# High and low parts of a stationary operand side by side, element by element, in the two gate-and-up stages of a decoder layer on one Trainium2 core

## The chip, the cores and the metric

The kernel runs on one core of one Trainium2 chip, in one launch. The metric is the device time of one execution in microseconds. Two runs of the kernel before took 2149.1 and 2149.21 us, with a median of 2149.15 us.

## The reference

One decoder layer on 256 tokens of width 2048, with 16 learned tokens put in front (272 positions). It has two SwiGLU feed-forward blocks around a mixer of attention and short convolution. Cut to what matters here:

```python
D_MODEL, SEQ, N_META, D_FF = 2048, 256, 16, 5632

def swiglu_ffn(h, w_gu, w_down):
    gate, up = jnp.split(h @ w_gu, 2, axis=-1)
    return (jax.nn.silu(gate) * up) @ w_down

    h = rms_norm(s, norm_ffn1)
    s = s + 0.5 * swiglu_ffn(h, ffn1_w_gu, ffn1_w_down)       # 272 positions
    ...                                                       # mixer, merged with w_gate, w_branch, w_out
    h = rms_norm(s, norm_ffn2)
    s = s + 0.5 * swiglu_ffn(h, ffn2_w_gu, ffn2_w_down)       # 256 positions are kept
    s = rms_norm(s, norm_final)
```

All inputs are float32, and the matrices `w_gu` are 2048 x 11264 in each feed-forward block.

## The kernel before, in words

**Products in two parts.** Every operand X of a large product is held as a high part (X rounded to the format float32r) and a low part (X less the high part, in the same format). A product A·B is three matmuls into one accumulator: high·high, low·high, high·low. ACT writes the high part of a weight tile (a copy that rounds), DVE subtracts it from the tile for the low part.

A matmul has a stationary operand of 128 x 128, loaded into the array before it, and a moving operand of 128 rows and up to 512 columns, streamed past it. In the trace each matmul is a pair: a weight load (PEld) and the matmul (PE). The load of the next matmul starts with the matmul that runs.

**First feed-forward block** (`gate_up`, L482, over `linear`, L305). The activations h1 move (272 columns, transposed: features on partitions), the weights are stationary. h1 is an `Act` (L174): eight tiles with two 128-row chunks each, in a tile the order is chunk, high or low, column. Each piece has room for 320 columns (`PIECE`), and the 272 sit at its end, so they start at column 48. The groups of 512 gate columns ("pg") and 512 up columns ("pu") alternate, 11 times each. One `linear` has 16 chunks; for each of them four blocks of 128 weight columns, and for each block three matmuls: L367 (high weights, high h1), L368 (high weights, low h1), L369 (low weights, high h1). Weights come 1 MB (four chunks) at a time by a DMA of SP's queue (L337), and are split two chunks at a time, one ACT copy of 128 x 1024 (L351) and one DVE subtraction (L356), into the tiles `wh` and `wl`. There are three buffers of each. So ACT waits until TensorE is done with the oldest one; nothing else sets the order there. The evictions of one linear run inside the next one (`flush` after its second chunk).

The down projection ("pd") is a `linear` too. Its activations are an `Apart` (L194): high and low parts in separate tiles of four chunks, 272 columns each, and its weight tiles start 16 or 48 columns into their buffers, with a chunk every 528 columns (`weights`, L209), so that weights and activations step in the same way.

**Second feed-forward block** (`gate_up_mix`, L686, over `linear_mix`, L549). Here the weights move (512 columns) and the activations h3 are stationary. h3 (L1100) is an `Act` as well, eight tiles for the eight pairs of chunks, 256 columns, without a lead: tiles 0 to 3 in buffers of 1088 columns (tag "act"), 4 to 7 in buffers of 1280 columns (tag "big"). A plan says for each pair of chunks which of two ways it goes: "D", eight products of a block of h3 with a weight tile, or "S", seven products as in Strassen's scheme, three of which take a block of h3 and four a sum of blocks (`sum_of_parts`, L523, and `combine`, L530, make these sums from the two parts). The plans are

```python
FFN2_FIRST = ("DDDDSSDS", (1,), {(3, 0): 4, (3, 1): 5, (6, 0): 7}, (4, 5))
FFN2 = ("DDSDSSDS", (1,), {(1, 1): 2, (3, 0): 4, (3, 1): 5, (6, 0): 7}, (2, 4, 5))
```

the first for the first of eleven groups, the second for the ten others. Each product is again three matmuls, L569 (high h3), L570 (low h3), L571 (high h3 with the low weights). The accumulators are "pg1" to "pg7" and "pgx", under the names pg and pgx in the trace.

h3 is made during the output projection ("pd" again in the names, 1356 to 1444 us): `turned` (L1117) transposes two chunks into PSUM, ACT multiplies by the gain into the high part (L1127), DVE makes the low part (L1128).

**The order of the work.** It is written out by hand in lists: `side` and `later` are taken at fixed chunks, `ahead` keeps the weight splits of `linear_tok` and `linear_mix` two tiles ahead of their products. None of it has costs or due times, and the change touches none of it.

Of the kernel before, what the change touches and what calls it, by code (L numbers as in the profile page):

```python
# [9 lines left out]
F32 = mybir.dt.float32  # L10
F32R = mybir.dt.float32r
# [4 lines left out]
P = 128  # L16
D = 2048
SEQ = 256
NMETA = 16
T = SEQ + NMETA  # L20
F = 5632
DC = D // P
GC = 4
GW = GC * P
W2 = D // 2
NH = 8
# [9 lines left out]
N_BIG = 8  # L36
PIECE = 320
# [17 lines left out]
DOWN = ("DDSDSDSD", (), {(1, 1): 2, (3, 1): 4, (5, 1): 6}, ())  # L55
DOWN_LAST = ("DDDSDS", (1,), {(2, 1): 3, (4, 1): 5}, ())
AHEAD = 2


@with_exitstack  # L60
def decoder_layer(ctx: ExitStack, tc: tile.TileContext, t, out):
    nc = tc.nc

    const = ctx.enter_context(tc.tile_pool(name="const", bufs=1))
    wpool = ctx.enter_context(tc.tile_pool(name="w", bufs=W_BUFS))
    apool = ctx.enter_context(tc.tile_pool(name="a", bufs=N_ACT))
# [4 lines left out]
    def bank(name):  # L71
        return psum.tile([P, 512], F32, tag="acc", name=name)
# [45 lines left out]
    def load_vectors():  # L118
# [12 lines left out]
        out=mask[:, T - P :],  # L131
        in_=mask[:, T - P :],
# [41 lines left out]
    class Act:  # L174


        def __init__(self, name, chunks, width, wide_slots=(), piece=None):
            self.width, self.lead = width, 0 if piece is None else piece - width
            self.tiles = []
            for g in range(chunks // 2):  # L180
                if g in wide_slots:
                    w = piece or width
                    raw = apool.tile([P, 4 * PIECE], F32R, tag="big", bufs=N_BIG, name=f"{name}{g}")
                    self.tiles.append(raw[:, : 4 * w].rearrange("p (c l w) -> p c l w", c=2, l=2))
                else:
                    self.tiles.append(apool.tile([P, 2, 2, width], F32R, tag="act", name=f"{name}{g}"))

        def both(self, c, t0, t1):
            return self.tiles[c // 2][:, c % 2, :, self.lead + t0 : self.lead + t1]

        def part(self, c, lo, t0, t1):
            return self.tiles[c // 2][:, c % 2, lo, self.lead + t0 : self.lead + t1]

    class Apart:  # L194

# [99 lines left out]
    def step(use, ring=True):  # L295

        ahead.append((use, ring))
        while sum(r for _, r in ahead) > AHEAD:
            ahead.pop(0)[0]()

    def drain():
        while ahead:
            ahead.pop(0)[0]()

    def linear(act, chunks, w, k0, c0, t0, t1, name, evict, before=None, side_at=(5, 9, 13), after=None, later_at=LATER_AT):  # L305

        n = t1 - t0
        kb = KB  # L310
        nl = LB * kb
        starts = list(range(0, len(chunks), kb))
        if before is not None:
            starts.insert(1, 1)
        acc = [bank(f"{name}_{j}") for j in range(GC)]
        ready = {}
        for b, b1 in zip(starts, starts[1:] + [len(chunks)]):
            blk = chunks[b:b1]
            r0 = (k0 + blk[0]) * P
            if isinstance(act, Apart):  # L320
                wh, wl = (
                    act.weights(wpool.tile([P, 2 * act.step + 2 * NMETA], F32R, tag=nm, name=nm), blk[0])
                    for nm in ("wh", "wl")
                )
            else:
                wh = wpool.tile([P, kb, GW], F32R, tag="wh", name="wh")
                wl = wpool.tile([P, kb, GW], F32R, tag="wl", name="wl")
            m = len(blk)
            if before is not None or b % nl == 0:
                st = wpool.tile([P, LB * kb, GW], F32, tag="st", bufs=ST_BUFS, name="st")  # L330
                ml = m if before is not None else min(nl, len(chunks) - b)
                with ExitStack() as order:
                    for ins in x_load:
                        order.enter_context(tc.issue_after(ins))
                    x_load.clear()
                    last_load[:] = [
                        nc.sync.dma_start(  # L337
                            out=st[:, :ml, :],
                            in_=w[r0 : r0 + ml * P, c0 : c0 + GW].rearrange("(c p) f -> p c f", p=P),
                        ).ins  # L340
                    ]
            sw = st[:, :m, :] if before is not None else st[:, b % nl : b % nl + m, :]
            with ExitStack() as order:
                if before is not None and b == 0:
                    with tc.issue_after(nc.scalar.copy(out=wh[:, :m, :], in_=sw).ins):
                        ready[0] = before(blk)
                if before is not None:
                    for ins in ready.pop(b):
                        order.enter_context(tc.issue_after(ins))
                if before is None or b:  # L350
                    nc.scalar.copy(out=wh[:, :m, :], in_=sw)  # L351
                if before is None and b:
                    for ins in ahead_of_split:
                        order.enter_context(tc.issue_after(ins))
                    ahead_of_split.clear()
                nc.vector.tensor_sub(wl[:, :m, :], sw, wh[:, :m, :].bitcast(F32))  # L356
            if before is not None and b1 < len(chunks):
                ready[b1] = before(chunks[b1 : starts[starts.index(b1) + 1] if b1 < starts[-1] else None])
            drain()
            for i, c in enumerate(blk):  # L360
                first, last = b + i == 0, b + i == len(chunks) - 1
                for j in range(GC):
                    a, f = acc[j][:, :n], slice(j * P, (j + 1) * P)
                    if 2 * n <= 512:
                        nc.tensor.matmul(acc[j][:, : 2 * n], wh[:, i, f], act.both(c, t0, t1), start=first, stop=False)
                    else:
                        nc.tensor.matmul(a, wh[:, i, f], act.part(c, 0, t0, t1), start=first, stop=False)  # L367
                        nc.tensor.matmul(a, wh[:, i, f], act.part(c, 1, t0, t1), start=False, stop=False)  # L368
                    nc.tensor.matmul(a, wl[:, i, f], act.part(c, 0, t0, t1), start=False, stop=last)  # L369
                if b + i == EVICT_AT:  # L370
                    flush()
                if b + i in later_at and later:
                    later.pop(0)()
                if b + i in side_at and side:
                    side.pop(0)()
                if after is not None:
                    after(b + i)
        flush()
        pending.append(lambda: evict(acc))

    def flush():
        while pending:
            pending.pop(0)()
# [123 lines left out]
    class Mixed:  # L507
# [7 lines left out]
        def sum(self, p, pool=None):  # L515

            f = tmp.tile([P, 2, SEQ], F32, tag="sc", name="sf")
            for k in range(2):
                c = 2 * p + k
                nc.vector.tensor_scalar_mul(f[:, k, :], s(c, NMETA), col(self.g0 + c))  # L520
            self.combine(p, f, pool)
# [189 lines left out]
        nc.vector.tensor_sub(tl[:, :, 1, :], f, tl[:, :, 0, :].bitcast(F32))  # L711


    h1 = Act("h1", DC, T, range(NH), PIECE)
    norm1 = Norm(0, "1")

    pm, split_of, turned = [], [], []
# [67 lines left out]
    for half in halves:  # L785
        m = gate_up(h1, half, t["ffn1_w_gu"][0], norm1, 0, before1 if half is halves[0] else None)
        if half is halves[0]:
            with tc.issue_after(last_load[0]):
                load_vectors()
        else:  # L790
            side.extend((make_vec, make_lam))
        for c in range(0, DC, GC):

            def down(pd, c=c, final=half is halves[-1]):
                for j in range(GC):
                    nc.vector.scalar_tensor_tensor(
                        out=s(c + j, 0), in0=pd[j][:, :T], scalar=0.5, in1=s(c + j, 0), op0=ALU.mult, op1=ALU.add
                    )
                    if final:
                        after1(c + j)  # L800

            linear(m, list(range(len(half) * GC)), t["ffn1_w_down"][0], half[0] * GC, c * P, 0, T, "pd", down)
# [265 lines left out]
    for d in range(D // GW):  # L1068
# [19 lines left out]
        if d < 2:  # L1088
            n = 3 * d
# [7 lines left out]
            side_at=(2, 5) if d == GC - 1 else range(2, NH),  # L1097
        )

    h3 = Act("h3", DC, SEQ, range(4, NH))  # L1100
    hn = Mixed(h3, G_FFN2, False)
    rtok3 = const.tile([P, 2], F32, name="rtok3")
    nss = const.tile([P, 2, 4], F32, name="nss")
# [139 lines left out]
    for half in thirds:  # L1243
        m = Act("m", len(half) * GC, SEQ, range(4))
# [3 lines left out]
        if final:  # L1248
            for q in range(2):
                nc.gpsimd.dma_start(  # L1250
                    out=gfin[q],
                    in_=t["norm_final"][q * W2 : (q + 1) * W2].rearrange("(o d) -> o d", o=1).to_broadcast([P, W2]),
                )
        ma = Mixed(m, 0, True)
        for u in range(2):
# [31 lines left out]
            chunks = list(range(len(half) * GC))  # L1287
# [43 lines left out]
```

## Time and profile before

| | |
|---|---|
| median of the runs | 2149.15 us (2149.1 and 2149.21) |
| span of the profiled execution | 2147.3 us |
| granted TensorE clock, mean | 0.999 |
| first feed-forward block, gate and up | 6.5 to 296.9 us and 439.8 to 676.6 us |
| second feed-forward block, gate and up | 1443.8 to 1612.9, 1698.2 to 1864.3, 1949.7 to 2074.0 us |
| DMA | 439.70 MB, mean 205 GB/s |

The execution that was profiled has no time of its own beside its span. The span is counted from the first to the last instruction of the program, and the runs' times are device times around it.

How to read the views: a row of grouped instructions has the line of the kernel, the engine, the operation, the tiles it writes and reads, the shape and the count; then the busy time in us and the mean duration of one in ns; then the idle time of the engine before them and what ended it. Matmuls overlap, so the duration of one (start to modelled end) is longer than the distance from one start to the next; that distance comes from a stretch of time and the number of matmuls that start in it. The counts of a table of stretches include instructions that reach over its edges.

### The profile page before, as it was taken

To read this page: it belongs to the slowest core of one execution; us is meant where nothing else is said; L and a number is where in the kernel's file an instruction comes from. 1 tells how busy PE (TensorE), PEld (TensorE's weight loads), DVE (VectorE), ACT (ScalarE), POOL (GpSimd) and SP (SyncE) were. 2 spreads that over 40 slices of the span, in tenths; PEclk is the share of its full clock that TensorE was granted. 3 is DMA by queue.
4 is the path that set the end of the run, shared out by engine and by line. 5 is a ranking of instruction groups with operands and counts; after the bars stand their busy time and mean duration, and the time that the engine had idled before them with its cause. 6 is when DMAs were issued, how large, how long until landed. Compare 5 with 4: busy or idle time off the path is not lost.

```text
span 2147.3 us, 33079 instructions
## 1 busy us (share of the span) xinstructions
PE 2137.4 (100%) x13202; PEld 1929.1 (90%) x13202; DVE 1611.9 (75%) x2139; ACT 1105.5 (51%) x1391; POOL 79.4 (4%) x89
## 2 busy tenths in 40 slices
PE   9999999999999999999999999999999999999998
PEld 9999999999999998899988888888888888888887
DVE  8555554445555668867887889889999899988998
ACT  6344443344333455545545555557665566555665
POOL 0000000000000000000000000001100111012100
PEclk9999999999999999999999999999999999999999
DMA  7555555555555555544455555668886999779963
GB/s 258 177 177 178 177 181 177 178 180 179 180 180 176 178 178 187 190 157 142 154 189 186 198 201 187 216 206 256 267 259 198 286 285 277 234 219 311 287 207 138
DMA packets 200544, 439.70 MB, mean 205 GB/s; under 512 B 10493, under 2 KB 11206, under 8 KB 200390
## 3 DMA queue, kind: packets, MB, share of 16 engines
q1 hardware_dynamic: 184022, 398.13, 54.9%
q0 software_dynamic: 15904, 38.80, 8.2%
q8 instruction: 103, 1.69, 0.3%
q10 hardware_dynamic: 464, 0.66, 0.1%
q14 instruction: 51, 0.42, 0.1%
HBM read 431.26 MB, written 2.10 MB: 202 GB/s over the span
## 4 chain that ended last, share of the span: by engine, by line
PE 98%; DVE 1%; DMA 0%; ACT 0%; issue 0%; SPq 0%; ACTq 0%
PE pg L569 6%; PE pg L571 6%; PE pg L570 6%; PE pd L369 4%; PE pd L367 4%; PE pu L367 4%; PE pu L368 4%; PE pu L369 4%; PE pd L368 4%; PE pg L367 4%; PE pg L368 4%; PE pg L369 4%; PE pd L571 4%; PE pd L570 4%; PE pd L569 4%; PE g L571 2%
## 5 line engine op out<-in xcount | busy, mean ns | idle before, releaser
L356 DVE TENSOR_TENSOR wl<-st,wh 128x1024 fp32r<-128x1024 f32 (+1 forms) x329 | 401.1, 1221 | 378.4 <-ACT wh L351 378.3
L351 ACT CAST wh<-st 128x1024 fp32r<-128x1024 f32 (+1 forms) x328 | 343.0, 1047 | 487.4 <-PE pu L368 151.0
L476 DVE TENSOR_TENSOR wl<-st,wh 128x1024 fp32r<-128x1024 f32 (+1 forms) x424 | 470.9, 1118 | 55.4 <-ACT wh L475 52.3
L475 ACT CAST wh<-st 128x1024 fp32r<-128x1024 f32 (+1 forms) x424 | 400.3, 970 | 208.8 <-PE pdx L570 60.5
L475 ACT CAST wh<-t 128x1024 fp32r<-128x1024 f32 x160 | 166.6, 1052 | 242.5 <-DVE t L609 162.3
L476 DVE TENSOR_TENSOR wl<-t,wh 128x1024 fp32r<-128x1024 f32 x160 | 193.8, 1222 | 56.3 <-ACT wh L475 51.7
L369 PE MATMUL pd<-mh,wl 128*128 128x272 f32 x704 | 203.1, 288 | 0.0
L367 PE MATMUL pd<-mh,wh 128*128 128x272 f32 x704 | 202.3, 287 | 0.0
L367 PE MATMUL pu<-h,wh 128*128 128x272 f32 x704 | 201.9, 287 | 0.0
L367 PE MATMUL pg<-h,wh 128*128 128x272 f32 x704 | 201.6, 287 | 0.2 <-ACT h L231 0.2
L369 PE MATMUL pu<-h,wl 128*128 128x272 f32 x704 | 201.7, 287 | 0.0
L368 PE MATMUL pu<-h,wh 128*128 128x272 f32 x704 | 201.7, 286 | 0.0
L368 PE MATMUL pg<-h,wh 128*128 128x272 f32 x704 | 201.2, 287 | 0.1
L368 PE MATMUL pd<-ml,wh 128*128 128x272 f32 x704 | 200.7, 285 | 0.0
L369 PE MATMUL pg<-h,wl 128*128 128x272 f32 x704 | 199.6, 287 | 0.1
L570 PE MATMUL pg<-wh,h 128*128 128x512 f32 x399 | 156.0, 391 | 0.0
L569 PE MATMUL pg<-wh,h 128*128 128x512 f32 x399 | 155.8, 390 | 0.0
L571 PE MATMUL pg<-wl,h 128*128 128x512 f32 x399 | 155.7, 391 | 0.0
L368 PEld LDWEIGHTS pd<-ml,wh 128*128 128x128 f32 x704 | 133.5, 190 | 0.0
L367 PEld LDWEIGHTS pg<-h,wh 128*128 128x128 f32 x704 | 132.6, 188 | 0.7 <-ACT h L231 0.4
L368 PEld LDWEIGHTS pg<-h,wh 128*128 128x128 f32 x704 | 132.6, 188 | 0.3 <-DVE h L232 0.3
L368 PEld LDWEIGHTS pu<-h,wh 128*128 128x128 f32 x704 | 132.6, 188 | 0.0
(391 smaller groups left out, 4839.6 us busy)
## 6 DMA issues: line engine op xcount, KB each, us to landing
st<-in_ffn_w_gu_dram SPq DMA_DIRECT2D x183, 512.0 KB, 6.0
st<-in_ffn_w_down_dram SPq DMA_DIRECT2D x88, 1024.0 KB, 5.1
st<-in_ffn_w_gu_dram SPq DMA_DIRECT2D x84, 1024.0 KB, 4.9
st<-in_w_in_dram SPq DMA_DIRECT2D x48, 1024.0 KB, 5.1
st<-in_w_gate_dram SPq DMA_DIRECT2D x64, 512.0 KB, 4.1
t<-in_ffn_w_gu_dram POOLq DMA_DIRECT2D x64, 512.0 KB, 7.0
st<-in_w_branch_dram SPq DMA_DIRECT2D x32, 512.0 KB, 4.5
st<-in_w_out_dram SPq DMA_DIRECT2D x16, 1024.0 KB, 5.2
```

The source lines that it names most:

```text
L351: nc.scalar.copy(out=wh[:, :m, :], in_=sw)
L356: nc.vector.tensor_sub(wl[:, :m, :], sw, wh[:, :m, :].bitcast(F32))
L367: nc.tensor.matmul(a, wh[:, i, f], act.part(c, 0, t0, t1), start=first, stop=False)
L368: nc.tensor.matmul(a, wh[:, i, f], act.part(c, 1, t0, t1), start=False, stop=False)
L369: nc.tensor.matmul(a, wl[:, i, f], act.part(c, 0, t0, t1), start=False, stop=last)
L475: part_last[:] = [nc.scalar.copy(out=wh, in_=src).ins]
L476: part_last.append(nc.vector.tensor_sub(wl, src, wh.bitcast(F32)).ins)
L569: nc.tensor.matmul(ps[k], hi, wh, start=first, stop=False)
L570: nc.tensor.matmul(ps[k], lo, wh, start=False, stop=False)
L571: nc.tensor.matmul(ps[k], hi, wl, start=False, stop=left[k] == 0)
```

## The change

The diff does four things.

1. In the up linears of the first block ("pu"), the weight tiles `wh` and `wl` have another content: one tile for each of the two chunks, and in it the high and the low part of each column next to each other. A stationary operand is then every second element of its tile (a step of 8 bytes). ACT copies and DVE subtracts once per chunk, with every second element written.
2. The eight tiles of h1 get leads of their own, 48, 0, 16, 32, 40, 8, 24 and 44 columns, instead of 48 for all.
3. The tiles of h3 get places: tiles 0 to 3 hold high and low parts element by element and start 0, 16, 32 and 48 columns into their buffers; tiles 4 to 7 keep their order and start 16, 32, 48 and 8 columns in. A column is 4 bytes.
4. `linear` loses the branch that put both parts of a narrow activation into one matmul, and names the two weight operands of a block first.

```diff
+LEADS = [48, 0, 16, 32, 40, 8, 24, 44]
+PLACES = [(0, True), (16, True), (32, True), (48, True), (16, False), (32, False), (48, False), (8, False)]
...
-        def __init__(self, name, chunks, width, wide_slots=(), piece=None):
-            self.width, self.lead = width, 0 if piece is None else piece - width
+        def __init__(self, name, chunks, width, wide_slots=(), piece=None, leads=None, places=None):
+            self.width = width
+            self.leads = leads or [0 if piece is None else piece - width] * (chunks // 2)
             self.tiles = []
             for g in range(chunks // 2):
-                if g in wide_slots:
+                if places is not None:
+                    first, mixed_parts = places[g]
+                    if g in wide_slots:
+                        raw = apool.tile([P, 4 * PIECE], F32R, tag="big", bufs=N_BIG, name=f"{name}{g}")
+                    else:
+                        raw = apool.tile([P, GC * T], F32R, tag="act", name=f"{name}{g}")
+                    raw = raw[:, first : first + 4 * width]
+                    how = "p (c w l) -> p c l w" if mixed_parts else "p (c l w) -> p c l w"
+                    self.tiles.append(raw.rearrange(how, c=2, l=2))
+                elif g in wide_slots:
...
         def part(self, c, lo, t0, t1):
-            return self.tiles[c // 2][:, c % 2, lo, self.lead + t0 : self.lead + t1]
+            lead = self.leads[c // 2]
+            return self.tiles[c // 2][:, c % 2, lo, lead + t0 : lead + t1]
...
+            elif name == "pu":
+                mixed_w = [wpool.tile([P, GW, 2], F32R, tag=nm, name=nm) for nm in ("wh", "wl")]
...
-                if before is None or b:
+                if name == "pu":
+                    for i in range(m):
+                        nc.scalar.copy(out=mixed_w[i][:, :, 0], in_=sw[:, i, :])
+                elif before is None or b:
                     nc.scalar.copy(out=wh[:, :m, :], in_=sw)
...
-                nc.vector.tensor_sub(wl[:, :m, :], sw, wh[:, :m, :].bitcast(F32))
+                if name == "pu":
+                    for i in range(m):
+                        nc.vector.tensor_sub(mixed_w[i][:, :, 1], sw[:, i, :], mixed_w[i][:, :, 0].bitcast(F32))
+                else:
+                    nc.vector.tensor_sub(wl[:, :m, :], sw, wh[:, :m, :].bitcast(F32))
...
-                    if 2 * n <= 512:
-                        nc.tensor.matmul(acc[j][:, : 2 * n], wh[:, i, f], act.both(c, t0, t1), start=first, stop=False)
+                    if name == "pu":
+                        whj, wlj = (mixed_w[i][:, f, k] for k in range(2))
                     else:
-                        nc.tensor.matmul(a, wh[:, i, f], act.part(c, 0, t0, t1), start=first, stop=False)
-                        nc.tensor.matmul(a, wh[:, i, f], act.part(c, 1, t0, t1), start=False, stop=False)
-                    nc.tensor.matmul(a, wl[:, i, f], act.part(c, 0, t0, t1), start=False, stop=last)
+                        whj, wlj = wh[:, i, f], wl[:, i, f]
+                    nc.tensor.matmul(a, whj, act.part(c, 0, t0, t1), start=first, stop=False)
+                    nc.tensor.matmul(a, whj, act.part(c, 1, t0, t1), start=False, stop=False)
+                    nc.tensor.matmul(a, wlj, act.part(c, 0, t0, t1), start=False, stop=last)
...
-    h1 = Act("h1", DC, T, range(NH), PIECE)
+    h1 = Act("h1", DC, T, range(NH), PIECE, leads=LEADS)
...
-    h3 = Act("h3", DC, SEQ, range(4, NH))
+    h3 = Act("h3", DC, SEQ, range(4, NH), places=PLACES)
```

More of the change, by code (lines that the diff above doesn't have):

```diff
@@ L188, in both @@
         def both(self, c, t0, t1):
-            return self.tiles[c // 2][:, c % 2, :, self.lead + t0 : self.lead + t1]
+            lead = self.leads[c // 2]
+            return self.tiles[c // 2][:, c % 2, :, lead + t0 : lead + t1]
         def part(self, c, lo, t0, t1):
-            return self.tiles[c // 2][:, c % 2, lo, self.lead + t0 : self.lead + t1]
+            lead = self.leads[c // 2]
+            return self.tiles[c // 2][:, c % 2, lo, lead + t0 : lead + t1]
     class Apart:
```

## The prediction

> **What bounds the kernel now.** I read the page's busy time and chain first, then the groups of instructions by line, then stretches of single stages, then the waits.
>
> ```profile
> span 2147.3 us, 33079 instructions
> ...
> PE 2137.4 (100%) x13202; PEld 1929.1 (90%) x13202; DVE 1611.9 (75%) x2139; ACT 1105.5 (51%) x1391; POOL 79.4 (4%) x89
> ...
> PE 98%; DVE 1%; DMA 0%; ACT 0%; issue 0%; SPq 0%; ACTq 0%
> ```
>
> TensorE is the path: 98% of the chain is PE. The span is 2147.3 us; the two runs shown have a median of 2149.15, so 1.85 us lie around the span. I make the sum as changes to the span and add them to 2149.2.
>
> So only the spacing of matmuls counts. The durations of single matmuls overlap and do not give it; stretches with a known count do. The first two rows below are one "pu" linear of the first FFN (16 chunks x 4 blocks x 3 products = 192 matmuls of 272 columns) and one "pd" linear (24 x 12 = 288); the third is the output projection, where h3 is made.
>
> ```profile
> core 0: us, PE busy (x) PEld busy (x) DVE busy (x) ACT busy (x) POOL busy (x), PEclk, DMA share, GB/s
> 83.79:107.47 23.68, 23.68 (x195) 23.68 (x193) 12.75 (x17) 9.49 (x12) 0.00 (x0) 1.00 0.54 178
> 332.63:368.35 35.72, 35.72 (x290) 35.72 (x289) 16.11 (x17) 12.61 (x12) 0.00 (x0) 1.00 0.52 177
> 1356.31:1443.77 87.46, 87.45 (x395) 71.41 (x393) 79.36 (x103) 49.55 (x65) 4.01 (x4) 1.00 0.67 211
> ```
>
> pu: 23.68 / 192 = 123.3 ns per matmul, 1.480 us per chunk of 12. pd: 35.72 / 288 = 124.0 ns, 1.488 us per chunk. Both have 272 columns, PE busy throughout and the full clock (1.00), yet pd loses 8.3 ns per chunk. What differs by the code is where the stationary operand that is being loaded lies against the moving operand that is streaming. I call the start of the moving operand minus the start of the next stationary one, modulo 128 bytes, the offset (taking tile starts as multiples of 128 bytes). In pu, h1 starts at 48 columns (192 bytes) and weights at multiples of 512: the offset is 64 in every matmul. In pd, the 64-byte steps of the two tiles keep it at 64 in 11 of 12 matmuls; the last of each chunk loads the next chunk's weights at 0. So one matmul at offset 0 costs up to 8.3 ns. In the second FFN:
>
> ```profile
> 1452.19 0.39 PE L571 MATMUL pgx<-wl,h 128*128 128x512 f32 x1
> ...
> 1454.69 0.39 PE L570 MATMUL pgx<-wh,h 128*128 128x512 f32 x1
> ```
>
> Eleven intervals in 2.50 us are 227 ns per matmul of 512 columns; there every operand starts on a multiple of 128 bytes, offset 0.
>
> **The change part by part.** How many matmuls each edit touches:
>
> ```profile
> L367 PE MATMUL pu<-h,wh 128*128 128x272 f32 x704 | 201.9, 287 | 0.0
> L367 PE MATMUL pg<-h,wh 128*128 128x272 f32 x704 | 201.6, 287 | 0.2 <-ACT h L231 0.2
> ...
> L570 PE MATMUL pg<-wh,h 128*128 128x512 f32 x399 | 156.0, 391 | 0.0
> ...
> L571 PE MATMUL pgx<-wl,h 128*128 128x512 f32 x90 | 35.1, 390 | 0.0
> ```
>
> pu and pg: 704 for each of three products, 2112 each. h3 is stationary in (399 + 90) x 3 = 1467 matmuls. A D pair has 24 of them, an S pair 9 (its other products use the sums). By the plans, the mixed pairs 0 to 3 have 96 in the first group and 81 in each of ten more: 906. The plain pairs 4, 5 and 7 have 99 each, pair 6 has 264: 561.
>
> *Leads of h1 in pg (contiguous weights).* The leads 48, 0, 16, 32, 40, 8, 24, 44 give offsets 64, 0, 64, 0, 32, 32, 96, 48. Two tiles stay at 64; six move. No row has a 272-column stage that is at offset 0 throughout, so the price per matmul there lies between 0 (a steady stream may settle) and 8.3 ns (pd's single ones). I take half, 4.2, for the two at 0 and a quarter, 2.1, for the four between: on the mean (2 x 4.2 + 4 x 2.1) / 8 = 2.1 ns, times 2112 = +4.4 us. Bounds 0 and 6/8 x 8.3 x 2112 = +13.1.
>
> *pu: the same leads, and strided loads.* The leads cost the same +4.4 (0 to +13.1). The load now takes every second element, 8 bytes apart. No row shows a strided load. Bounds come from the surcharge that a matmul pays beside its columns. If offsets 0 and 64 cost the same, a column takes (227 - 123.3) / 240 = 0.432 ns, 272 take 117.5, and the surcharge is 5.8 ns for both widths. If 272 columns at offset 0 take 123.3 + 8.3 = 131.6, a column takes 0.397 ns, and the surcharge is 15.2 ns in pu and 23.5 in the 512s. The middles are 10.5 and 14.7. The strided load may save all of it or pay it a second time (a load then spans twice the bytes): -32 to +32 us in pu, -21 to +21 for the 906. I take 0, because the sign is open and the nearest row, the contiguous load, is all the trace has.
>
> [...]
>
> *h3's places.* Pairs 1, 3 (mixed, 264 each), 4 (99) and 6 (264) go from offset 0 to 64, 891 matmuls; pair 7 (99) to 96; pairs 0, 2 and 5 stay. With the same 4.2 and 2.1: -(891 x 4.2 + 99 x 2.1) = -4.0 us; bounds 0 and -8.2.
>
> *Elementwise work.* Each block of two chunks in pu has one ACT cast and one DVE subtraction of 1024 elements; now two of 512.
>
> ```profile
> L356 DVE TENSOR_TENSOR wl<-st,wh 128x1024 fp32r<-128x1024 f32 x327 | 399.7, 1224 | 378.4 <-ACT wh L351 378.3
> L351 ACT CAST wh<-st 128x1024 fp32r<-128x1024 f32 x327 | 342.4, 1048 | 487.4 <-PE pu L368 151.0 <-PE pd L368 147.7 <-PE pg L368 125.2
> L475 ACT CAST wh<-st 128x512 fp32r<-128x512 f32 x80 | 49.1, 614 | 0.0
> L476 DVE TENSOR_TENSOR wl<-st,wh 128x512 fp32r<-128x512 f32 x80 | 54.7, 684 | 0.0
> ```
>
> ```profile
> ACT wh L351 <- PE pu L368: 151.0, 86, 2.0
> ```
>
> ACT: 2 x 614 - 1048 = +180 ns, DVE: 2 x 684 - 1224 = +144 ns per block, 88 blocks: +15.8 and +12.7 us of work. It lies under PE: in a pu linear ACT is busy 9.49 and DVE 12.75 of 23.68 us, and ACT waited 151 us for PE to free a weight buffer, so the split runs ahead. Cost 0; without cover at most those 15.8. Buffers, loads and queues are as before; no wait is added, and one buffer comes free a chunk earlier. h3's 16 casts and 16 subtractions, and one sum of parts, become partly strided:
>
> ```profile
> L1127 ACT ACTIVATE h<-h_ps,vec 128x256 fp32r<-128x256 f32 x16 | 7.2, 468 | 2.5 <-DVE h L1128 2.5
> L1128 DVE SCALAR_TENSOR_TENSOR h<-h_ps,vec,h 128x256 fp32r<-128x256 f32 x16 | 7.4, 478 | 0.2 <-ACT h L1127 0.2
> ```
>
> Were the eight of each that are mixed to take twice as long, that is 8 x 0.48 = 3.8 us of DVE, where the output projection leaves 87.46 - 79.36 = 8.1. Cost 0, at most +3.8. The removed branch for 2n <= 512 was never taken (n is 272 or 258).
>
> Sum: 2149.2 + 4.4 + 4.4 - 4.0 = 2154.
>
> **The rivals.**
>
> *In step (faster).* If the surcharge comes from the two streams meeting in the memory as one overtakes the other, a load with twice the stride could run at the moving stream's pace, slip once and not meet it again. For it: an offset matters at all (pd). Against: nothing shows the pace of a load. Saving two thirds of the middles, 7.0 x 2112 + 9.8 x 906 = 14.8 + 8.9, with +4.4 for pg and -1.7 for the plain h3 pairs: 2149.2 - 21.0 = 2128.
>
> *Twice the meetings (slower, under 2%).* Twice the bytes spanned, the surcharge paid once more: 10.5 x 2112 + 14.7 x 906 = 22.2 + 13.3 on top of the forecast: 2154 + 35.5 = 2189.
>
> *The load becomes the bound (the other side).* Each load starts with one matmul and has to be done for the next, so it fits into 123.3 ns now. If a stride of two halves its rate, it sets the spacing in pu as soon as it passes 123.3 ns.
>
> ```profile
> L369 PEld LDWEIGHTS pu<-h,wl 128*128 128x128 f32 x704 | 132.6, 188 | 0.0
> ```
>
> From 188 (a load's own row) to 2 x 123.3 = 246.7 ns: +64.7 to +123.4 ns, 2112 times, +137 to +261 us; the 227 of the 512s covers it but for 0 to 18 us. That is 2291 to 2433, say 2360. For it: the row is longer than the spacing already. Against: nothing in the trace shows a load waiting on memory. [...]
>
> *Strided elementwise writes.* If ACT and DVE took twice as long on them, DVE in a pu linear would have 12.75 + 8 x (2 x 2 x 0.684 - 1.224) = 24.8 us in 23.68: it would set the pace by 1.1 us in 11 linears, 2154 + 13 = 2167 at most.
>
> *Nothing happens.* If places in the memory don't matter for PE and pd's 8.3 ns has another cause (its high and low parts lie in two tiles), the time is 2149. [...]
>
> **How the numbers follow.** Forecast 0.40, in step 0.25, twice the meetings 0.18, load as the bound 0.07, elementwise 0.04, nothing 0.06. The predicted time is 2154. The range goes from 2122 (in step, somewhat better than its middle) to 2195 (twice the meetings, somewhat worse); left out are the load as the bound, 0.07, a third of twice the meetings, 0.06, and a quarter of in step, 0.06. 2% is 43 us, about what a measurement of this kernel can tell from no change. Slower by more: 0.07 and the 0.06, 0.13. Faster by more needs -43: only in step with the highest surcharge, 0.02. Within: 0.85.
>
> **What would show it.** Right: a pu and a pg linear of about 24.1 us each (chunks of 1.48 to 1.58, by tile), tiles with leads 48 and 16 unchanged in pg, h3's pairs 1 and 3 faster than 227 ns and pairs 0 and 2 at 227; ACT still waiting on PE in pu. In step: pu under 23 us at nearly all leads. Twice the meetings: pu over 25.5. Load as the bound: pu from 36 us. Elementwise: PE idle before pu's weight loads, released by DVE. The forecast is wrong in its mechanism if a pu tile with lead 48 or 16 differs from 1.480 us per chunk: then the stride has a price of its own.

## The result and the profile after

The changed kernel takes 2167.03 us (2166.96 and 2167.11), the kernel before 2149.15: 1.0084 times as long, 95% interval 1.0054 to 1.0113. That is 0.8% slower, clear of the noise (the two runs of each kernel agree within 0.2 us), and inside the range. The forecast was 2154.0; 13 of the 17.9 us were not foreseen.

The page of the changed kernel (span, busy time, chain):

```profile
span 2165.3 us, 33262 instructions
...
PE 2154.6 (100%) x13202; PEld 1944.4 (90%) x13202; DVE 1623.4 (75%) x2227; ACT 1127.5 (52%) x1479; POOL 79.4 (4%) x89
...
PE 98%; DVE 1%; ACT 0%; DMA 0%; issue 0%; SPq 0%; ACTq 0%
```

TensorE is the path as before, with the same 13202 matmuls and loads; it is busy 17.2 us longer (2137.4 before). Nothing waits in its place (the waits listed for TensorE come to 2.4 us, before to 1.8), so the matmuls stand further apart. To see which ones, take stretches from the first matmul of a stage to the first of the next. TensorE is busy throughout each, so the length of the stretch is the reading. Before, a pg linear, the down projection's 1152 matmuls, and the three gate-and-up stages of the second feed-forward block (the pu linear stands in the prediction):

```profile
core 0: us, PE busy (x) PEld busy (x) DVE busy (x) ACT busy (x) POOL busy (x), PEclk, DMA share, GB/s
60.11:83.79 23.68, 23.68 (x195) 23.68 (x193) 12.52 (x15) 9.67 (x11) 0.00 (x0) 1.00 0.54 179
296.91:439.79 142.88, 142.88 (x1155) 142.88 (x1154) 65.73 (x67) 51.54 (x50) 0.00 (x0) 1.00 0.52 177
1443.77:1612.89 169.12, 169.12 (x765) 139.30 (x763) 160.82 (x206) 110.99 (x137) 17.70 (x18) 1.00 0.83 258
1698.21:1864.33 166.12, 166.12 (x746) 137.35 (x745) 152.19 (x174) 102.93 (x117) 22.54 (x23) 1.00 0.90 275
1949.65:2073.99 124.34, 124.34 (x557) 102.82 (x556) 113.36 (x130) 76.78 (x87) 16.69 (x17) 1.00 0.91 280
```

After, the same stages in the same order, with a pu linear as the second row:

```profile
61.08:85.09 24.01, 24.01 (x194) 24.01 (x193) 12.62 (x16) 9.32 (x13) 0.00 (x0) 1.00 0.52 174
85.09:109.31 24.22, 24.22 (x194) 24.22 (x193) 13.56 (x23) 11.88 (x19) 0.00 (x0) 1.00 0.55 176
302.25:445.13 142.88, 142.88 (x1155) 142.88 (x1154) 65.50 (x66) 50.60 (x49) 0.00 (x0) 1.00 0.53 177
1453.58:1625.49 171.91, 171.91 (x764) 141.69 (x763) 161.36 (x206) 110.98 (x137) 17.67 (x18) 1.00 0.82 253
1710.80:1880.07 169.27, 169.27 (x745) 139.58 (x744) 152.74 (x174) 102.89 (x117) 22.52 (x23) 1.00 0.90 269
1965.38:2092.09 126.71, 126.71 (x557) 104.49 (x556) 113.80 (x130) 76.76 (x87) 16.67 (x17) 1.00 0.89 274
```

A pg linear takes 0.33 us more, a pu linear 0.54 more (24.22 - 23.68), the three stages of h3 take 2.79, 3.15 and 2.37 more; the down projection takes the same 142.88. Over all linears: pg +3.2, pu +6.3, h3 +8.3, together 17.8 of the span's 18.0 us. The clock is 1.00 in every row.

The elementwise work went as forecast. ACT and DVE in that pu linear, by shape, and what ACT waited for there:

```profile
L377 DVE TENSOR_TENSOR wl<-st,wl 128x512 fp32r<-128x512 f32 x6 | 4.1, 691 | 3.3 <-ACT wl L368 3.3
L368 ACT CAST wl<-st 128x512 fp32r<-128x512 f32 x6 | 4.0, 664 | 4.0 <-PE pu L393 4.0
```

```profile
ACT wl L368 <- PE pu L393: 4.0, 5, 0.9
```

The strided writes cost 691 and 664 ns where the plain ones of the same size had 684 and 614. ACT still waits for TensorE to free a weight buffer, so the split still runs ahead.

The weight loads themselves became a little longer, 195 ns in place of the 188 of the contiguous ones:

```profile
L391 PEld LDWEIGHTS pu<-h,wl 128*128 128x128 f32 x32 | 6.2, 195 | 0.0
```

The starts of the matmuls give the spacing tile by tile. I measure a place by what I call the distance: the start of the moving operand minus the start of the next stationary one, modulo 256 bytes (the prediction used 128). It is worked out from the kernel's code and takes every buffer to start at a multiple of 256 bytes, which no trace shows; the differences between two places of one buffer do not depend on that. The 272-column linears, in ns per matmul (a chunk's 12 matmuls, from the first to the first of the next chunk, over 12; median over the linears, second chunk of the tile):

| lead of h1 | 48 | 0 | 16 | 32 | 40 | 8 | 24 | 44 |
|---|---|---|---|---|---|---|---|---|
| distance | 192 | 0 | 64 | 128 | 160 | 32 | 96 | 176 |
| pg, contiguous weights | 123.3 | 125.0 | 126.7 | 126.7 | 123.3 | 126.1 | 126.7 | 123.3 |
| pu, every second element | 126.7 | 124.4 | 126.1 | 126.7 | 126.7 | 126.0 | 126.7 | 126.5 |

In pg, lead 16 differs from lead 48, though both are at 64 modulo 128; in pu, lead 48 isn't at 123.3. The prediction had named both tiles as its test. The tiles run one behind the other, each right behind another place, so an entry can carry something over from the tile before it; of the contiguous places, only leads 48 and 16 were also run alone.

### The profile page after: what moved, and what is told of

The parts are those of the page before. It is cut to its first block, busy times and chain, and to the rows that moved or that the text cites. A ratio compares the mean times of both kernels' runs of the same rounds, so it can differ in the third digit from the quotient of the medians.

```text
span 2165.3 us, 33262 instructions
## 1 busy us (share of the span) xinstructions
PE 2154.6 (100%) x13202; PEld 1944.4 (90%) x13202; DVE 1623.4 (75%) x2227; ACT 1127.5 (52%) x1479; POOL 79.4 (4%) x89
## 4 chain that ended last, share of the span: by engine, by line
PE 98%; DVE 1%; ACT 0%; DMA 0%; issue 0%; SPq 0%; ACTq 0%
PE pg L593 6%; PE pg L595 6%; PE pg L594 6%; PE pd L393 4%; PE pu L393 4%; PE pu L391 4%; PE pd L391 4%; PE pu L392 4%; PE pd L392 4%; PE pg L392 4%; PE pg L391 4%; PE pg L393 4%; PE pd L595 4%; PE pd L593 4%; PE pd L594 4%; PE g L595 2%
## 5 line engine op out<-in xcount | busy, mean ns | idle before, releaser
L500 DVE TENSOR_TENSOR wl<-st,wh 128x1024 fp32r<-128x1024 f32 (+1 forms) x424 | 471.2, 1119 | 56.6 <-ACT wh L499 53.6
L499 ACT CAST wh<-st 128x1024 fp32r<-128x1024 f32 (+1 forms) x424 | 400.3, 969 | 213.0 <-PE pdx L594 59.0
L379 DVE TENSOR_TENSOR wl<-st,wh 128x1024 fp32r<-128x1024 f32 (+1 forms) x241 | 293.3, 1219 | 277.1 <-ACT wh L370 238.4
L370 ACT CAST wh<-st 128x1024 fp32r<-128x1024 f32 (+1 forms) x240 | 251.1, 1047 | 361.3 <-PE pd L392 149.6
L391 PEld LDWEIGHTS pd<-mh,wh 128*128 128x128 f32 x704 | 132.4, 188 | 0.1
L393 PEld LDWEIGHTS pd<-mh,wl 128*128 128x128 f32 x704 | 132.3, 188 | 0.0
L393 PEld LDWEIGHTS pg<-h,wl 128*128 128x128 f32 x704 | 131.3, 188 | 0.5 <-DVE wl L379 0.5
L377 DVE TENSOR_TENSOR wh<-st,wh 128x512 fp32r<-128x512 f32 x88 | 60.9, 692 | 62.5 <-ACT wh L368 62.5
```

Source lines behind the costliest of these rows:

```text
L377: nc.vector.tensor_sub(mixed_w[i][:, :, 1], sw[:, i, :], mixed_w[i][:, :, 0].bitcast(F32))
L391: nc.tensor.matmul(a, whj, act.part(c, 0, t0, t1), start=first, stop=False)
L393: nc.tensor.matmul(a, wlj, act.part(c, 0, t0, t1), start=False, stop=last)
L499: part_last[:] = [nc.scalar.copy(out=wh, in_=src).ins]
L500: part_last.append(nc.vector.tensor_sub(wl, src, wh.bitcast(F32)).ins)
```

## The experiments

Each result is a single run beside a run of the kernel before on the same chip (2148.9 to 2149.2 us), and one profile. Most effects are below a microsecond per linear, so the verdicts come from the length of stages in the traces. Three theories stood against each other:

- Theory 1: the place counts, with another period than 128 bytes, and a strided load has a price of its own.
- Theory 2, the prediction's: only the place modulo 128 bytes counts, and the stride is free.
- Theory 3, formed after the first runs: TensorE settles into one of a few regular spacings and stays in it until something disturbs it; place and stride decide which ones can be held.

Diffs are against the changed kernel.

**One part at a time.** Only the leads:

```diff
-            elif name == "pu":
+            elif name == "none":
...
-    h3 = Act("h3", DC, SEQ, range(4, NH), places=PLACES)
+    h3 = Act("h3", DC, SEQ, range(4, NH))
```

> Only the eight leads of h1; the up weights and h3 as before. Theory 1 (the changed kernel's own tiles: a contiguous load has a spacing by where it lies modulo 256 bytes, and a strided load has a price of its own): pg 24.01 us per linear as in the changed kernel, and pu the same 24.01 in place of 24.22, so +0.33 in each of 22 linears, +7.2 us on the span of 2147.3. Theory 2 (the recorded forecast: places alone count, the stride is free): pu keeps the 24.22 of the changed kernel, +9.6 us in all. Second feed-forward block as before in both.

2157.87 us, +8.7. A pg and the next pu linear:

```profile
60.76:84.77 24.01, 24.01 (x194) 24.01 (x193) 12.44 (x15) 9.70 (x11) 0.00 (x0) 1.00 0.54 176
84.77:108.89 24.12, 24.12 (x195) 24.12 (x194) 12.84 (x18) 9.51 (x12) 0.00 (x0) 1.00 0.54 175
```

+0.33 and +0.44 us, close to the prediction's 0.4 a linear. But pg and pu are the same code here, and they differ; after the first down projection they change roles (pg 24.11, pu 24.02). At leads 24 and 44 the linears of 24.02 us have 126.7 and 123.3 ns per matmul, those of 24.11 have 125.2 and 126.7: one place, two spacings. So here a linear's time depended on what ran before it.

Only the strided load in pu, all leads at 48:

```diff
-LEADS = [48, 0, 16, 32, 40, 8, 24, 44]
+LEADS = [48, 48, 48, 48, 48, 48, 48, 48]
...
-    h3 = Act("h3", DC, SEQ, range(4, NH), places=PLACES)
+    h3 = Act("h3", DC, SEQ, range(4, NH))
```

> Only the up weights element by element; all eight leads 48, h3 as before. Theory 1 (a strided load has a price of its own, about 3.3 ns per matmul, the 1.520 against 1.480 us per chunk of the tile with lead 48 in the changed kernel): pu 16 x 1.520 = 24.3 us, pg 23.68, +7.0 us. Theory 2 (only places count): pu 23.68, no change. If the elementwise work were late, PE would be idle ahead of pu's weight loads.

2159.88 us, +10.7. A pg and a pu linear in the first half, and another pair in the second:

```profile
60.92:84.61 23.69, 23.69 (x194) 23.69 (x193) 12.61 (x16) 9.33 (x13) 0.00 (x0) 1.00 0.53 176
84.61:109.14 24.53, 24.53 (x195) 24.53 (x193) 13.59 (x23) 11.88 (x19) 0.00 (x0) 1.00 0.55 174
492.87:517.19 24.32, 24.32 (x195) 24.32 (x193) 12.64 (x17) 9.38 (x13) 0.00 (x0) 1.00 0.51 171
517.19:541.51 24.32, 24.32 (x195) 24.32 (x193) 13.61 (x23) 11.83 (x19) 0.00 (x0) 1.00 0.55 177
```

With nothing else changed, the strided load costs 24.32 to 24.53 against 23.68 us: 3.3 to 4.4 ns per matmul. Theory 2 falls. And in the second half pg takes 24.32 us as well, in all but its first linear, although nothing in pg was touched.

Only the starts of h3's tiles, parts apart; and only the mixed parts of tiles 0 to 3, all starts at 0:

```diff
-PLACES = [(0, True), (16, True), (32, True), (48, True), (16, False), (32, False), (48, False), (8, False)]
+PLACES = [(0, False), (16, False), (32, False), (48, False), (16, False), (32, False), (48, False), (8, False)]
```

> Only the starts of h3's tiles, with high and low parts apart as before. Theory 1 (for 512 moving columns a start at a multiple of 256 bytes is the best, any other costs 2 to 7 ns): the second feed-forward block's three gate-and-up stages +5 to +6 us in all. Theory 2 (recorded: 64 bytes better than 0): -2 to -4 us.

```diff
+PLACES = [(0, True), (0, True), (0, True), (0, True), (0, False), (0, False), (0, False), (0, False)]
```

> Only h3's tiles 0 to 3 element by element, all eight tiles at the start of their buffers as before. Theory 1 (a strided load has its own price, 232 to 233 against 226.7 ns in the changed kernel): 906 matmuls x 5.5 to 6.5 ns, +5 to +6 us in the three gate-and-up stages of the second block. Theory 2 (only places count): no change.

Both with plain pu and leads at 48. 2155.17 (+6.0) and 2154.31 us (+5.2). The stages of h3 in the first of them:

```profile
1443.81:1614.95 171.14, 171.14 (x765) 139.52 (x763) 161.06 (x206) 111.03 (x137) 17.67 (x18) 1.00 0.82 254
1700.27:1868.69 168.42, 168.42 (x745) 137.52 (x744) 152.55 (x174) 102.94 (x117) 22.55 (x23) 1.00 0.89 270
1954.01:2080.12 126.11, 126.11 (x557) 102.94 (x556) 113.64 (x130) 76.81 (x87) 16.67 (x17) 1.00 0.90 276
```

+2.02, +2.30 and +1.77: 6.1 us for the places alone; the mixed parts alone give 1.93, 2.01 and 1.53, 5.5 us. Single matmuls show the spacing. Tile 0, which starts at distance 0 in both kernels, contiguous in the first and every second element in the second:

```profile
1443.81 0.39 PE L593 MATMUL pg<-wh,h 128*128 128x512 f32 x1
...
1446.53 0.39 PE L593 MATMUL pg<-wh,h 128*128 128x512 f32 x1
```

```profile
1444.28 0.39 PE L594 MATMUL pg<-wh,h 128*128 128x512 f32 x1
...
1446.85 0.39 PE L595 MATMUL pg<-wl,h 128*128 128x512 f32 x1
```

12 intervals in 2.72 us are 226.7 ns, 11 in 2.57 are 233.6. With parts apart, by distance: 226.7 ns at 0, some 233 to 234 at 192 and 128, 229 at 64, 232 at 224. So for 512 columns, distance 0 is the best of these places, and the stride at distance 0 cost as much (6.9 ns) as the worst of them (some 7). In the changed kernel the mixed tiles have about 230 to 234 ns and the plain ones 229 to 234: a tile that is both strided and displaced pays about once, which is why 6.1 and 5.5 make 8.3.

**The period.** All leads at 16, nothing else. By the prediction's modulo 128 this is the place of lead 48:

```diff
+LEADS = [16, 16, 16, 16, 16, 16, 16, 16]
```

> All eight leads of h1 are 16 columns (64 bytes) in place of 48 (192 bytes); weights and h3 as before. The distance between the moving and the loaded operand is then 64 modulo 128 as before, but 64 and not 192 modulo 256. If 128 bytes are the period (the recorded working): pg and pu 23.68 us, no change. If 256 is (tiles 0 and 2 of the kernel with the leads alone, both at 64 modulo 128, took 1.480 and 1.520 us per chunk): 16 x 1.520 = 24.3 us in each of 22 linears, +14 us.

2162.22 us, +13.2. A pg and a pu linear:

```profile
60.49:84.81 24.32, 24.32 (x194) 24.32 (x193) 12.51 (x15) 9.78 (x11) 0.00 (x0) 1.00 0.53 174
84.81:109.13 24.32, 24.32 (x194) 24.32 (x193) 12.79 (x18) 9.51 (x12) 0.00 (x0) 1.00 0.53 173
```

Each linear costs 0.64 us more, all but the very first, which waits for its inputs: 21 x 0.64 = 13.4 us. The same code, the same instructions, other addresses: 126.7 instead of 123.3 ns. Distances 64 and 192 differ, so the period is not 128.

All runs with leads move the moving operand alone, and all runs with h3 the stationary one alone. That the place of one against the other counts, and not the start of the moving operand by itself, follows from the down projection of the kernel before. By its code the moving operand starts at 0, 64, 128 and 192 bytes modulo 256 in four chunks in turn, and the weights step along. If the start alone counted, its chunks would differ as leads 0, 16, 32 and 48 do (123.3 to 126.7 ns); in the trace all 96 take 1.485 to 1.489 us, 124 ns per matmul.

**One linear alone.** All leads at 48, and only the first up linear of the second half (after the first down projection) is element by element:

```diff
-            elif name == "pu":
+            elif name == "pu" and c0 == F + 6 * GW:
```

> The up weights are element by element in a single linear, the first up linear of the second half; all leads 48. Where all up linears had mixed weights, the gate linears of the second half, whose own weights and places were unchanged, ran at 24.32 us, and those of the first half at 23.69. Theory 1 (places and stride set the spacing of each matmul by themselves): that linear 24.3 us, every other 23.68, +0.6 us. Theory 3 (TensorE settles into one of a few regular spacings and keeps it until something disturbs it): the gate and up linears after it stay at 24.3 us although nothing in them differs from the kernel before, 8 more linears, up to +5.8 us, until the down projection.

2154.94 us, +6.0, from one linear in 22. The pg before it, the changed pu, the pg after it, and the last pu of the block:

```profile
439.75:463.43 23.68, 23.68 (x195) 23.68 (x193) 11.55 (x15) 10.37 (x13) 0.00 (x0) 1.00 0.55 179
463.43:487.75 24.32, 24.32 (x195) 24.32 (x193) 13.55 (x23) 11.90 (x20) 0.00 (x0) 1.00 0.56 175
487.75:512.07 24.32, 24.32 (x195) 24.32 (x193) 12.33 (x14) 8.86 (x10) 0.00 (x0) 1.00 0.51 172
657.99:682.31 24.32, 24.32 (x195) 24.32 (x193) 12.79 (x18) 9.51 (x12) 0.00 (x0) 1.00 0.51 174
```

The changed linear is slower by 0.64 us, and so is each of the eight that follow, though they are as in the kernel before: 9 x 0.64 = 5.8 us. The down projection behind them takes 119.49 us, 119.46 before. This is what theory 3 said: the slower spacing was entered in the strided linear and kept where the faster one would have held as well. The weight loads of the eight are contiguous and take 188 ns, as in the kernel before, so a longer load is not what keeps it.

**A kick.** If the spacing is only kept, a disturbance could end it. The same kernel, with two float32 matmuls of 128 columns, whose result nobody reads, in the middle of the next pg linear:

```diff
+                if name == "pg" and c0 == 7 * GW and b + i == 8:
+                    kick = bank("kick")
+                    for _ in range(2):
+                        nc.tensor.matmul(kick[:, :P], ones, ones, start=True, stop=True)
```

> The single mixed up linear again, and in the gate linear after it, at chunk 8, two float32 matmuls of 128 columns into a bank that nothing reads. If the slower spacing is only a regular pattern that TensorE keeps until something disturbs it, the kick lets it settle anew: gate and up linears after it at 23.68 us again, where they were at 24.32 without the kick, so the time is about 4.9 us under that of the kernel without it (2154.9), near 2150.2. If the places of the operands alone set the spacing, or something else in the second half is slower, they stay at 24.32 and the time at 2155.

2150.41 us, +1.5: 4.5 less than without the kick. Single matmuls around it (the two float32 matmuls stand as four in the trace):

```profile
499.31 0.29 PE L392 MATMUL pg<-h,wl 128*128 128x272 f32 x1
...
501.21 0.29 PE L392 MATMUL pg<-h,wl 128*128 128x272 f32 x1
501.33 0.61 PE L398 MATMUL kick<-ones 128*128 128x128 f32 x4
...
502.16 0.29 PE L390 MATMUL pg<-h,wh 128*128 128x272 f32 x1
...
504.38 0.28 PE L390 MATMUL pg<-h,wh 128*128 128x272 f32 x1
```

15 intervals in 1.90 us before the kick, 126.7 ns; 18 in 2.22 after it, 123.3. The linear with the kick and the next one:

```profile
487.66:512.15 24.49, 24.49 (x199) 24.49 (x197) 12.25 (x14) 8.75 (x10) 0.00 (x0) 1.00 0.51 171
512.15:535.83 23.68, 23.68 (x195) 23.68 (x193) 12.80 (x17) 9.61 (x12) 0.00 (x0) 1.00 0.54 179
```

Two controls. The kernel before with the same kick:

> The kernel before with the same two matmuls at the same place and nothing mixed: the control. If 123.3 ns is what a disturbance leads to at lead 48, all linears stay at 23.68 us and the kick costs its own time, 0.3 to 0.7 us. If a disturbance can as well throw it into the slower pattern, the linears after it go to 24.32, +5.4 us.

2150.95 us, +2.1. All later linears stay at 23.68; the one with the kick takes 0.46 us more. The rest of the 2.1 us does not lie at the kick: the first matmul starts 0.9 us later, and the last gate-and-up stage takes 0.5 us more. And all leads at 16, with the kick:

> All leads 16 with nothing mixed, as in the run that took 24.32 us per linear, and the kick of two float32 matmuls at chunk 8 of the same gate linear. If the slower spacing there is only a pattern that it fell into, the kick frees it as it did at lead 48: the linears after it at 23.68 us, about 4.5 us less than the 2162.2 without the kick. If a distance of 64 modulo 256 can't hold the faster spacing, they stay at 24.32 and the time at 2162 to 2163.

2162.94 us, +13.8. The linear with the kick, and the next one:

```profile
495.30:520.06 24.76, 24.76 (x199) 24.76 (x197) 12.47 (x15) 9.78 (x11) 0.00 (x0) 1.00 0.52 171
520.06:544.38 24.32, 24.32 (x195) 24.32 (x193) 12.79 (x18) 9.51 (x12) 0.00 (x0) 1.00 0.54 174
```

Here the kick changes nothing behind it. At distance 192 both spacings were held (123.3 and 126.7 ns), at 64 of these two only the slower one was seen.

**A step of four elements.** The nearest thing to the rival in which the load becomes the bound: the same bytes with a step of four elements (16 bytes) in pu, leads at 48:

```diff
-                mixed_w = [wpool.tile([P, GW, 2], F32R, tag=nm, name=nm) for nm in ("wh", "wl")]
+                mixed_w = [wpool.tile([P, GW // 2, 4], F32R, tag=nm, name=nm) for nm in ("wh", "wl")]
```

> Up weights with high and low parts of two chunks side by side, so that a stationary operand takes every fourth element (16 bytes apart, 2048 bytes in all); twice as many ACT and DVE instructions of half the size per block; leads 48, h3 as before. If a load slows with the lines it touches, as with one used element per 16 bytes, it sets the spacing: 188 ns or more per matmul, pu 36 us or more, +136 us. If each doubling of the spread adds what the first did (3.3 ns): pu 25 us, +14 us. If only the regular spacings seen so far exist (123.3, 126.7, 127.8): pu 24.3 to 24.5 us as with a step of two.

2381.38 us, +232.4. A pg and a pu linear:

```profile
81.13:104.81 23.68, 23.68 (x193) 23.68 (x193) 13.42 (x18) 10.44 (x15) 0.00 (x0) 1.00 0.42 138
104.81:149.61 44.80, 44.80 (x194) 44.80 (x193) 20.52 (x38) 17.91 (x32) 0.00 (x0) 1.00 0.35 116
```

44.80 / 192 = 233.3 ns per matmul, with TensorE never idle and ACT and DVE busy less than half the time. The loads of this linear grew with it:

```profile
L399 PEld LDWEIGHTS pu<-h,wh 128*128 128x128 f32 x32 | 10.5, 329 | 0.0
```

A load takes 329 ns in place of 188, and a matmul comes 110 ns later. From these numbers I take the load to set the pace here; a matmul's wait for its load was not shown. With a step of 8 bytes a load takes 193 to 200 ns, but the spacing does not follow it: at distance 192 it is 3.3 to 4.4 ns longer than with contiguous loads, at distance 0 up to 0.9 shorter.

**Other places.** Is there one that beats 192 in pg or 0 in h3? Plain operands, eight new leads and eight new starts of h3:

```diff
+LEADS = [0, 4, 12, 20, 28, 36, 38, 42]
+PLACES = [(4, False), (60, False), (2, False), (56, False), (12, False), (52, False), (1, False), (44, False)]
```

> No operand is mixed; other places, to look for better ones. Leads of h1: 0, 4, 12, 20, 28, 36, 38, 42 columns (0 to 168 bytes); starts of h3's tiles: 4, 60, 2, 56, 12, 52, 1, 44 columns, so distances of 240, 16, 248, 32, 208, 48, 252 and 80 modulo 256. By what the leads alone showed: tiles of h1 at 144 to 168 bytes near 1.480 us per chunk, those from 0 to 112 between 1.49 and 1.52, pg and pu about 24.0 us. For h3, 64 to 224 took 229 to 235 ns against 226.7 at 0: places within 16 bytes of 0 should be at 227 and the others above 228. If any takes less than 226.7 or 123.3, a faster kernel is to be had from it.

2164.39 us, +15.4. In ns per matmul of 272 columns in pu (second chunk of each tile): distance 0: 125.6; 16: 124.8; 48: 125.0; 80: 125.0; 112: 123.3; 144: 124.4; 152: 126.7; 168: 128.9. Of 512 columns, within 1 ns: 240 and 16: 227; 80 and 248: 230 to 231; 48, 252, 208 and 32: 232 to 234. Two expectations failed. Leads at 144 to 168 bytes were to be near 123.3 ns, but 152 and 168 are the slowest of the row, while 112, which was to be slower, has 123.3. And distances 252 and 248 in h3, 4 and 8 bytes from 0, were to be at 227 ns and take 232 and 231. None is faster than the place in the kernel before, and no kernel here beats it.

**The strided load at another place.** All of pu element by element, all leads 0, so that pg and pu have the same distance 0:

```diff
+LEADS = [0] * 8
```

> All up linears mixed, all leads 0. In the changed kernel the tile with lead 0 took 1.493 to 1.496 us per chunk with mixed weights, and 1.500 to 1.508 with plain ones. If that holds for all tiles: pu 23.9 us (less than the 24.3 to 24.5 at lead 48: a strided load has its best place elsewhere), pg 24.0 to 24.1. If the strided load costs 1.520 wherever the pattern has time to settle: pu 24.3, pg 24.1 to 24.3.

2156.39 us, +7.5. A pg (contiguous) and a pu (strided) linear:

```profile
157.27:181.34 24.07, 24.07 (x195) 24.07 (x194) 12.65 (x16) 9.37 (x13) 0.00 (x0) 1.00 0.52 174
181.34:205.24 23.90, 23.90 (x195) 23.90 (x193) 13.56 (x23) 11.89 (x19) 0.00 (x0) 1.00 0.55 178
```

At distance 0 the strided load is the faster one: 124.5 against 125.4 ns. At 192 it is the slower one, 126.7 against 123.3. So the stride had no fixed price in these two places; it changed which of them is good. (No run has plain weights at distance 0 throughout, so the 125.4 may be partly carried over from the strided linear before; the mixed sequences of the other runs have 125.0 to 125.6 there.) The first pu linears of this kernel took 24.54 and 24.32 us before it came to 23.90, again a state that was left late.

**What it comes to.** Theory 2 fell (lead 16; strided at 192). Theory 1 holds in part: the place counts beyond 128 bytes, but the price of the stride has either sign (+3.3 ns at 192, -0.9 at 0). Theory 3 is shown for 272 columns by the one linear and the kicks. The parts do not add up: the leads, the strided load, and h3's two edits cost 8.7 + 10.7 + 6.0 + 5.2 = 30.6 us one by one and 17.9 together. Some 3.3 us of the difference are h3's tiles, which pay about once. For the rest, this is the likely account, put together from the runs and not tested by one of its own: in the run with the strided load alone, all leads are at a place that is bad for it, and pg is carried into the slow spacing for four of its eleven linears; with the eight leads the place changes every two chunks, pg comes back to 123.3 in three tiles of eight, and pu meets distance 0, where it is better off.

What stays open: why these spacings and no others, that is, what in the memory or the array they come from; what lets a linear leave the slow one (with the strided load alone, pg comes back to 23.69 us behind strided linears of 24.53 in the first half, and stays at 24.32 behind those of 24.32 in the second); whether the period is 256 bytes or longer (no pair of places 256 apart was tried); why 168 is so much worse than 160 and 176; and pd's 8.3 ns per chunk, for which no other place was tried.

## Why the prediction was right, and where it was wrong

- *What bounds the kernel, and that only the spacing counts:* right. TensorE has 98% of the chain before and after; 17.8 of 18.0 us are in the pg, pu and h3 stages, which the edits touch, and the down projection, which they do not, takes the same 142.88 us.
- *Leads in pg, +4.4:* +3.2 measured, +0.33 in nearly every linear. The size was near by luck, for the step behind it was wrong: "modulo 128 bytes". Lead 16 was counted as free and takes 126.7 ns; leads 40 and 44 were counted with 2.1 ns and have 123.3 here.
- *The same leads in pu, +4.4, and the strided load, 0:* +6.3 measured for both, and +4.3 for the leads alone. "I take 0, because the sign is open": the sign was open indeed. The same load cost 3.3 ns at distance 192 and saved 0.9 at 0. Alone at the old leads it cost 0.64 to 0.85 us a linear; with the new leads the two are not a sum. The bounds of 32 us stood for 15.2 ns per matmul; the most that the stride of two cost is 4.4: the surcharge as a whole was neither saved nor doubled.
- *h3's places, -4.0:* the step that failed most. +6.1 by themselves, +8.3 with the mixed tiles, for which 0 had been taken. The working moved pd's price for offset 0 at 272 columns, 8.3 ns for a single matmul within a chunk, to 512 columns; there 0 is as good as any place tried; only the places 16 bytes to either side come within 1 ns of it, and all others cost 2 to 7. The steady stream of the 512s at distance 0 stood in the trace at 227 ns, but with nothing beside it to say that it was good or bad; the sign was an inference, and the bounds "0 and -8.2" had left the other sign out without a reason.
- *Elementwise work, 0:* right, with 11.88 and 13.56 us of ACT and DVE under 24.22 of TensorE. The rival *strided elementwise writes* gave "2167 at most", which is the measured time by chance only: DVE took 691 ns and not twice 684, and TensorE was busy throughout the pu linear shown. Only 8 of h3's 16 casts run in the output projection, the other 8 in the first stage of h3, in both kernels.
- *In step, 2128:* out; the fastest strided linear seen is 23.90 us, and no place or stride tried came under 123.3 and 226.7 ns. *Twice the meetings, 2189:* out; pu would be over 25.5 us. *The load becomes the bound:* not at 8 bytes; at 16, as I read it, with 233.3 ns, within the bounds 188 to 246.7 given for it. *Nothing happens:* out; moving the running operand by 128 bytes against the loaded one took a linear from 23.68 to 24.32 us.

So of the four terms two had the wrong rule and came out near, one (the stride) had been left open, and one had the wrong sign. The time lay in the range because the price of a place was a few ns in every run (0 to 5.6 over 123.3 for 272 columns), whatever its rule, and because the range, 2122 to 2195, is wide: that is luck more than understanding. What no reading of this trace could give is that rule: before, nearly every matmul of a width stood at one place, so the trace held one point of the curve, and pd's single matmuls, one in twelve, from which I drew the second, do not show what a place costs that every matmul of a stream has.

## What to carry to other kernels

In a stream of matmuls that never idles, the place of the moving operand against the stationary one that is being loaded was worth 2 to 5% of the spacing here, with a best place that differed with the width (for 272 columns 192 with 123.3 ns, where 0 had 125.0 to 125.6; for 512 columns 0 with 226.7, where 192 had 233 to 234) and with the stride (0 was better than 192 for a strided load, 124.5 against 126.7); try a few starts on the chip before choosing a layout, and give a price from one width or one place no sign at another. Read a stage by its length from first matmul to first matmul, and compare it with an untouched stage behind it: here eight linears took 24.32 us in place of 23.68 because of the one before them. When parts that are tried alone cost more than all of them together (30.6 us against 17.9 here), look for a state that is carried over, and test it with a disturbance.

## What the runs showed of the hardware that was not expected

- Matmuls of 272 columns with a load for each ran at 123.3 or 126.7 ns with the same instructions and places. One strided linear left the eight behind it at the slower spacing (8 x 0.64 = 5.1 us); in another run two short float32 matmuls ended it (24.32 to 23.68 us).
- A stationary operand of every second float32 cost 3.3 ns over 123.3 at distance 192 and was 0.9 ns faster than a contiguous one at distance 0 (124.5 against 125.4); its load took 193 to 200 ns, a contiguous one 188. With every fourth the load took 329 ns and the spacing was 233.3.
